# Two branch pairs of a recurrent mixer in seven products instead of eight, with the residual reloaded later

## The chip, the cores and the metric

The kernel runs on one core of a Trainium2 chip. TensorE (PE) multiplies matrices: it holds a 128x128 block of weights and streams a moving operand of up to 512 columns past it, into PSUM. VectorE (DVE) and ScalarE (ACT) do the elementwise work and are the only ones here that take results out of PSUM. GpSimd (POOL) and SyncE (SP) issue DMA transfers, each from its own queue. Every engine takes its instructions in the order of its queue and waits on semaphores for the others. The metric is device time in microseconds (us), lower is better.

## The reference

A decoder layer on 512 tokens of width 1024, in float32: a SwiGLU feed-forward (width 2816), then a mixer, then a second feed-forward, each between RMSNorms and added to the residual `h`. The mixer projects the normed input `u` once and runs two branches side by side:

```
u = rms_norm(h, mix_norm_pre)
q, k, v, xr, yr, gl = split(u @ w_in)          # xr, yr: width 1024
attn_d = dilated_attention(q, k, v) @ w_attn_branch
xc  = causal_conv4(xr) + conv_b
gate_x, gate_a = sigmoid(xc @ w_x + b_x), sigmoid(xc @ w_a + b_a)   # 4 heads of 256
a   = exp(-8 * gate_a * softplus(-a_param))
h_t = a_t * h_{t-1} + sqrt(1 - a_t^2) * gate_x * xc
rec = h_t * gelu(yr)
merged = sigmoid(gl0) * attn_d + sigmoid(gl1) * (rec @ w_rec_branch)
h = h + rms_norm(merged @ w_out, mix_norm_post)
```

The change is about `yr = u @ w_in[yr columns]`, for the first two of the four heads.

## The kernel before, in words

Precision. Every float32 operand is kept as two parts, high and low (`split`, lines 283 to 285: ACT writes the rounded high part, DVE the difference). A product is three matmuls, high x high, high x low, low x high (`mm3`, lines 297 to 299).

Weights. All weights come as one stream in order of use (`stream_plan`), in raw loads of up to 2048 columns (1 MB) into two `raw` buffers, issued by SP (line 230). `fetch` splits a tile of 128 output columns (1024 wide in memory) into one of four `w8` buffers, or a half-size one into one of two `w4` buffers.

A plain column tile is `gemm`: 8 blocks of the contraction x 3 = 24 matmuls of 128x512 into one of five PSUM tiles `acc`.

A pair of column tiles can be done in seven products (a Strassen-Winograd scheme): input and weights are cut into 2x2 quarters, the contraction in two halves and the tokens in two halves of 256, and seven products p1 to p7 of sums of quarters replace eight. A product (`seventh`, lines 616 to 618) is 4 blocks x 3 = 12 matmuls of 128x256. The forms of the input are made once per stage (`forms_of`): p1, p2, p3 are views of `u` itself, p5 and p7 lie in buffers of the pool that also holds the residual, p6 and p4 in `tx` buffers of the attention pool. The forms of the weights are made per pair by `w_forms`: with raw quarters u0, u1, g0, g1 it makes u0+u1, u0+u1+g0, u0+g0 and u0+u1+g0+g1 on DVE (512 wide each) and splits three tiles of 1024 and one of 512: one for p1 and p2 (raw g), one for p6 and p5 (the first two sums), one for p7 and p4, one for p3. Two evaluations exist: `seven`, whose results are added on DVE, and `seven_on`, which accumulates in PSUM and copies partial sums on ACT (line 631). The feed-forwards, the q/k projections and the gate of the attention branch use them.

The recurrent stage. After attention come four gate pairs (`seven`), then the attention product of eight tiles (contraction 512: 12 matmuls each), then the recurrent stage in an order written out by hand:

```
LRU_ORDER = (("conv", 0), ("branch", 0), ("branch", 1), ("conv", 1), ("gates", 0), ("branch", 2), ("conv", 2),
             ("gates", 1), ("gate1", 1), ("branch", 3), ("gates", 2), ("conv", 3), ("gate1", 2), ("gates", 3),
             ("gate1", 3))
```

`conv` of a head is two plain tiles, each evicted by DVE (line 1269), run through four taps (lines 1270 to 1272) and split into `rec`. `branch` is two plain tiles, evicted by DVE into `ge` (line 1286); after every second head ACT applies Gelu to four of them (line 1292). `gates` is the small per-head product on `rec`, and `recur` the recurrence. `rec` takes 32 KB per partition, `sig` 16 KB. Constants of the recurrence are made from `a_param` by a chain of small DVE operations and one Exp (lines 1237 to 1252).

The residual was stored in DRAM (`kept_m`) and is loaded back by POOL in four transfers of 512 KB after the last gate pair, ahead of the attention product (line 1216). It is used after the output product, much later.

Who sets the order: the program is written as one stream; a scheduler orders each engine's queue by priority, which `high_priority` raises (`AHEAD` for weight preparation, `EVAC` for evictions), and adds the waits. A new pool that lies over the memory of pools that were closed is writable when those are no longer read.

Of the kernel before, what the change touches and what calls it, by code (L numbers as in the profile page):

```python
# [10 lines left out]
F32 = mybir.dt.float32  # L11
F32R = mybir.dt.float32r
AF = mybir.ActivationFunctionType
ALU = mybir.AluOpType
# [25 lines left out]
CB = 6  # L40
GATE1 = ((), (0, 1), (2, 3, 4), (5, 6, 7))

LRU_ORDER = (("conv", 0), ("branch", 0), ("branch", 1), ("conv", 1), ("gates", 0), ("branch", 2), ("conv", 2),
             ("gates", 1), ("gate1", 1), ("branch", 3), ("gates", 2), ("conv", 3), ("gate1", 2), ("gates", 3),
             ("gate1", 3))

# [37 lines left out]
def part_blocks(a):  # L84

    return (FF_PARTS[a][1] - FF_PARTS[a][0]) // 2


def stream_plan():
# [36 lines left out]
    for h in range(NH):  # L126
        qk(h)
    for c in range(0, KC, 2):
        plan.append((("pair", 52 + c, 53 + c), 2048))
    for m in range(KC):  # L130
        plan.append((("attn", m), 512))
    for what, h in LRU_ORDER:
        if what == "gates":
            plan.append((("lru", h), 1024))
        else:
            cs = GATE1[h] if what == "gate1" else (2 * h, 2 * h + 1)
            o = {"conv": 36, "branch": 44, "gate1": 60}[what]
            for c in cs:
                plan.append((("in", o + c), 1024))
# [32 lines left out]
def hybrid_layer(ctx: ExitStack, tc: tile.TileContext, xT: bass.AP, xN: bass.AP, wst: bass.AP,  # L172
# [365 lines left out]
    def tx_slot(pool, bufs=1):  # L538
        return pool.tile([P, 2, 4, HB], F32R, name="tx", tag="tx", bufs=bufs)

    def forms_of(x, his, los, pool, copied):


        spool[0] = pool
# [2 lines left out]
        def quarter(i, j):  # L547
            return fx[:, 2 * j:2 * j + 2, i * T:i * T + T]

        def slot():  # L550
# [37 lines left out]

    spool = [None]

    def w_forms(key):

        with tc.high_priority(offset=AHEAD):
            raw = raw_of(key)
            u0, u1, g0, g1 = (raw[:, i * 512:(i + 1) * 512] for i in range(4))
            s12 = spool[0].tile([P, 2, 512], F32, name="s12", tag="s", bufs=2)
            DVE.tensor_add(s12[:, 1, :], u0, u1)  # L597
            DVE.tensor_add(s12[:, 0, :], s12[:, 1, :], g0)
            DVE.tensor_add(u0, u0, g0)
# [17 lines left out]
            PE.matmul(ps, wh, xl, start=False, stop=False, skip_group_check=True)  # L617
            PE.matmul(ps, wl, xh, start=False, stop=k == 3, skip_group_check=True)  # L618

    def seven_on(t, w, g, u):  # L620

        b, z, y, v = (acc_ps()[:, :HB] for _ in range(4))
        lo, hi = HALVES

        def copy(ps, dst=None):
            if dst is None:
                dst = tpool.tile([P, HB], F32, name="c", tag="c", bufs=CB)
            with tc.high_priority(offset=EVAC):  # L630
                ACT.activation(dst, ps, AF.Copy)  # L631
            return dst

        def sum_of(dst, ps, c):
            with tc.high_priority(offset=EVAC):
                DVE.tensor_add(dst, ps, c)
# [52 lines left out]
    def ffn(n, x, r, forms_x, apool, pss):  # L689
# [101 lines left out]
        def prod(f, w):  # L791
            g, u = tmp("g"), tmp("u")
            if f >= FIRST_ON[n]:
                v = seven_on(t, w, g, u)

                def put(dst, view):
                    for q, (h, src) in enumerate(zip(HALVES, (v, u[:, HALVES[1]]))):
                        DVE.scalar_tensor_tensor(dst[:, q] if len(dst.shape) == 3 else dst[:, h], g[:, h], -1.0, src,
                                                 op0=ALU.mult, op1=ALU.mult)
                into(f, put)  # L800
# [192 lines left out]
    ff1.close()  # L993


    with ExitStack() as mx:
        tpl = mx.enter_context(tc.tile_pool(name="attn_out", bufs=1))
        apool_cm = tc.tile_pool(name="attention", bufs=1)
# [51 lines left out]
        t, steps = forms_of(um, um_t[:2], um_t[2:], apool, False)  # L1050
# [170 lines left out]

    with ExitStack() as mx:
        rpool = mx.enter_context(tc.tile_pool(name="rec", bufs=1))
        rec_t = rpool.tile([P, 16, T], F32R, name="rec")
        rec = Act([rec_t[:, i, :] for i in range(8)], [rec_t[:, 8 + i, :] for i in range(8)])
        sig = rpool.tile([P, KC, T], F32, name="sig")
        lpool_cm = tc.tile_pool(name="lru", bufs=1)
        lpool = lpool_cm.__enter__()

# [27 lines left out]
        def pi(ap):  # L1257
            return ap.rearrange("q (p i) -> q p i", p=4)

        def conv(hd):  # L1260

            for c in (2 * hd, 2 * hd + 1):
# [109 lines left out]
        for c in range(KC):  # L1372
# [5 lines left out]
            DVE.tensor_mul(sig[:, c, :], ps, sig[:, c, :])  # L1378
            DVE.tensor_add(sig[:, c, :], sig[:, c, :], facc[:, c, :])
            split(mg.hi[c], mg.lo[c], sig[:, c, :])  # L1380


    ap2 = ctx.enter_context(tc.tile_pool(name="act2", bufs=1))
# [141 lines left out]
```

## Time and profile before

| | |
|---|---|
| median of 3 runs | 1227.53 us (1226.97 to 1227.96) |
| the profiled execution | 1227.1 us |
| its span, first to last instruction | 1225.3 us |
| granted TensorE clock, mean | 0.999 |
| busy: PE, weight loads, DVE, ACT, POOL | 99%, 90%, 80%, 64%, 2% |
| DMA, mean | 121 GB/s |

A row of the order in time is: start in us from the span's start, duration, engine, line, operation, what is written from what, shape, count; in brackets the idle time of the engine before it and what ended that. PE is the matmul, PEld the weight load that overlaps it, and SPq and POOL rows are DMA issues. Matmul durations overlap: the spacing of their starts is what a matmul costs in a row of them. "x2" merges neighbours.

### The profile page before, as it was taken

The page shows a single profiled execution, that of the slowest core. Times are in us where ns is not written, and L with a number is a line of the kernel's source. Part 1 is how long each engine was busy: PE and PEld are TensorE (multiplying, and loading weights), DVE is VectorE, ACT ScalarE, POOL GpSimd, SP SyncE. Part 2 cuts the span into 40 slices and gives each one's busy share as a digit, 9 for nine tenths or more (in the row PEclk, how much of TensorE's full clock was granted, in tenths as well). Part 3 has the DMA queues.
Part 4 walks back from the last instruction along what each step waited for, and adds up shares of the span by engine and source line. Part 5 has one row for each costly group of instructions (what it writes and reads, how often), then busy time and mean ns, then how long its engine had stood idle before and what let it go on. Part 6 is the DMA issues. An engine that isn't in the chain of part 4 may idle for free.

```text
span 1225.3 us, 19182 instructions
## 1 busy us (share of the span) xinstructions
PE 1214.1 (99%) x7700; PEld 1102.8 (90%) x7700; DVE 981.5 (80%) x1497; ACT 784.0 (64%) x1337; POOL 26.1 (2%) x51
## 2 busy tenths in 40 slices
PE   9999999999999999999999999999999999999997
PEld 8899999999878899999988888888899999999996
DVE  7988888899677587888565897785798888889975
ACT  7556777777555365665543888844566677878752
POOL 0000000000002000000000000000100000000000
PEclk9999999999999999999999999999999999999999
DMA  6223333334614222222252222234453333333341
GB/s 246 89 84 121 121 121 121 121 121 167 245 69 146 89 93 103 79 78 103 73 204 74 98 104 74 98 110 168 151 156 121 121 120 121 121 120 121 138 172 69
DMA packets 29401, 148.73 MB, mean 121 GB/s; under 512 B 3200, under 2 KB 6400, under 8 KB 15232
## 3 DMA queue, kind: packets, MB, share of 16 engines
q1 hardware_dynamic: 22032, 130.20, 29.4%
q0 software_dynamic: 7280, 17.30, 4.1%
q8 instruction: 60, 0.98, 0.3%
q14 instruction: 29, 0.24, 0.1%
HBM read 137.01 MB, written 6.29 MB: 117 GB/s over the span
## 4 chain that ended last, share of the span: by engine, by line
PE 93%; DVE 3%; ACT 2%; DMA 1%; issue 0%; DVEq 0%; ACTq 0%
PE acc L616 14%; PE acc L617 14%; PE acc L618 14%; PE acc L297 8%; PE acc L298 8%; PE acc L299 8%; PE aux L879 3%; PE aux L880 3%; PE aux L881 3%; PE acc L403 2%; PE acc L405 2%; PE acc L404 2%; PE acc L1025 1%; PE acc L1027 1%; PE acc L1026 1%; DMA raw<-in_w 1%
## 5 line engine op out<-in xcount | busy, mean ns | idle before, releaser
L285 DVE TENSOR_TENSOR w<-raw,w 128x1024 fp32r<-128x1024 f32 (+1 forms) x274 | 296.3, 1086 | 75.8 <-ACT w L284 68.8
L616 PE MATMUL acc<-big,w 128*128 128x256 f32 x1208 | 342.8, 284 | 0.4 <-ACT c L631 0.4
L617 PE MATMUL acc<-big,w 128*128 128x256 f32 x1208 | 342.7, 284 | 0.0
L618 PE MATMUL acc<-big,w 128*128 128x256 f32 x1208 | 342.4, 283 | 0.0
L284 ACT ACTIVATE w<-raw 128x1024 fp32r<-128x1024 f32 (+1 forms) x274 | 258.5, 949 | 120.1 <-PE acc L299 36.7
L616 PEld LDWEIGHTS acc<-big,w 128*128 128x128 f32 x1208 | 231.5, 192 | 2.4 <-ACT c L631 1.0
L617 PEld LDWEIGHTS acc<-big,w 128*128 128x128 f32 x1208 | 231.6, 192 | 1.4
L618 PEld LDWEIGHTS acc<-big,w 128*128 128x128 f32 x1208 | 231.6, 192 | 0.0
L616 PE MATMUL acc<-tx,w 128*128 128x256 f32 x276 | 78.5, 284 | 0.0
L617 PE MATMUL acc<-tx,w 128*128 128x256 f32 x276 | 78.1, 283 | 0.0
L618 PE MATMUL acc<-tx,w 128*128 128x256 f32 x276 | 78.1, 283 | 0.0
L879 PE MATMUL aux<-w,xf 128*128 128x512 f32 x196 | 76.4, 393 | 0.8 <-ACT w L284 0.8
L880 PE MATMUL aux<-w,xf 128*128 128x512 f32 x196 | 76.6, 391 | 0.0
L881 PE MATMUL aux<-w,xf 128*128 128x512 f32 x196 | 76.3, 389 | 0.0
L297 PE MATMUL acc<-big,w 128*128 128x512 f32 x192 | 74.7, 389 | 0.0
L298 PE MATMUL acc<-big,w 128*128 128x512 f32 x192 | 74.7, 389 | 0.0
L299 PE MATMUL acc<-big,w 128*128 128x512 f32 x192 | 74.7, 389 | 0.0
L284 ACT ACTIVATE w<-s 128x1024 fp32r<-128x1024 f32 x53 | 56.0, 1058 | 19.7 <-PE acc L618 13.9
L285 DVE TENSOR_TENSOR w<-s,w 128x1024 fp32r<-128x1024 f32 x53 | 64.6, 1218 | 4.2 <-ACT w L284 4.2
L597 DVE TENSOR_TENSOR s<-raw 128x512 f32<-128x512 f32 x53 | 36.4, 687 | 32.7 <-DMA raw<-in_w 32.7
L616 PEld LDWEIGHTS acc<-tx,w 128*128 128x128 f32 x276 | 52.9, 192 | 0.1
L617 PEld LDWEIGHTS acc<-tx,w 128*128 128x128 f32 x276 | 52.9, 192 | 0.0
(367 smaller groups left out, 2572.2 us busy)
## 6 DMA issues: line engine op xcount, KB each, us to landing
raw<-in_w SPq DMA_DIRECT2D x110, 1024.0 KB, 4.8
raw<-in_w SPq DMA_DIRECT2D x14, 512.0 KB, 3.6
big<-xf POOLq DMA_DIRECT2D x6, 512.0 KB, 3.2
gains<-in_rows POOLq DMA_DIRECT2D x5, 512.0 KB, 4.9
h<-in_x SPq DMA_DIRECT2D x8, 256.0 KB, 5.1
h<-in_xn POOLq DMA_DIRECT2D x4, 512.0 KB, 5.6
kept_m<-h POOLq DMA_DIRECT2D x4, 512.0 KB, 2.9
h<-kept_m POOLq DMA_DIRECT2D x4, 512.0 KB, 5.2
```

Of the source, the lines that this page charges most:

```text
L284: ACT.activation(dh, src, AF.Copy)
L285: DVE.tensor_sub(dl, src, dh.bitcast(F32))
L297: PE.matmul(ps, wh, xh, start=first, stop=False)
L298: PE.matmul(ps, wh, xl, start=False, stop=False)
L299: PE.matmul(ps, wl, xh, start=False, stop=last)
L597: DVE.tensor_add(s12[:, 1, :], u0, u1)
L616: PE.matmul(ps, wh, xh, start=start and k == 0, stop=False, skip_group_check=True)
L617: PE.matmul(ps, wh, xl, start=False, stop=False, skip_group_check=True)
L618: PE.matmul(ps, wl, xh, start=False, stop=k == 3, skip_group_check=True)
L879: PE.matmul(ps, xh, wh, start=first and j == 0, stop=False, skip_group_check=True)
L880: PE.matmul(ps, xh, wl, start=False, stop=False, skip_group_check=True)
L881: PE.matmul(ps, xl, wh, start=False, stop=j == 1, skip_group_check=True)
```

## The change

1. `LRU_ORDER` begins with branch 0 and branch 1, then conv 0, conv 1; the rest is as it was.
2. These two branches (`PAIRED`) are each a pair in seven products, `seven_on`, on the input forms that attention made. Their raw weights come as pairs of 2048 columns, the same bytes. `seven_on` now takes functions for its four results; the feed-forward passes its old ones, the branch copies two quarters on ACT (one with the sign turned) and adds two on DVE.
3. The first pair's weight forms are asked for behind the attention product, the second's at the head of the first branch. Their two sums use parts of `sig`, not a buffer of the closed attention pool.
4. So that the forms outlive attention, p6 and p4 of the input lie in a new pool `keep` (16 KB per partition) instead of `tx`. After the two pairs the same memory holds the second half of `rec`.
5. p5 and p7 stay in the buffers that the residual wants; its reload moves behind the two pairs.

```diff
-LRU_ORDER = (("conv", 0), ("branch", 0), ("branch", 1), ("conv", 1), ("gates", 0), ("branch", 2), ("conv", 2),
+LRU_ORDER = (("branch", 0), ("branch", 1), ("conv", 0), ("conv", 1), ("gates", 0), ("branch", 2), ("conv", 2),
...
+PAIRED = LRU_ORDER[:2]
...
         if what == "gates":
             plan.append((("lru", h), 1024))
+        elif (what, h) in PAIRED:
+            plan.append((pair_key(what, h), 2048))
...
         def slot():
-            return tx_slot(pool, 1 if copied else 2).rearrange("p s k t -> p s (k t)").rearrange(
-                "p s (b c) -> p s b c", b=2)
+            if not copied and not two:
+                v = rb()
+                two.extend(v[:, 4 * i:4 * i + 4, :].rearrange("p (s j) t -> p s j t", s=2) for i in range(2))
+            if two:
+                return two.pop(0)
+            return tx_slot(pool).rearrange("p s k t -> p s (k t)").rearrange("p s (b c) -> p s b c", b=2)
...
-    def w_forms(key):
+    def w_forms(key, s12=None):
...
-            s12 = spool[0].tile([P, 2, 512], F32, name="s12", tag="s", bufs=2)
+            if s12 is None:
+                s12 = spool[0].tile([P, 2, 512], F32, name="s12", tag="s", bufs=2)
...
-    def seven_on(t, w, g, u):
+    def seven_on(t, w, g0, g1, u0, u1):
...
         seventh(t, w, "p2", y, False)
-        ACT.activation(g[:, lo], y, AF.Silu)
+        g0(y)
         seventh(t, w, "p7", b, False)
         copy(b, v)
-        sum_of(u[:, hi], b, c5)
+        u1(b, c5)
         seventh(t, w, "p3", z, False)
-        sum_of(g[:, hi], z, c6)
-        ACT.activation(g[:, hi], g[:, hi], AF.Silu)
+        g1(z, c6)
         seventh(t, w, "p4", v, False)
-        return v
+        u0(v)
...
+    kpool_cm = tc.tile_pool(name="keep", bufs=1)
+    kpool = kpool_cm.__enter__()
+    def rec_half():
+        return kpool.tile([P, 8, T], F32R, name="rb", tag="rb")
...
-        new_h()
-        for b in range(4):
-            nc.gpsimd.dma_start(hb(b), kept_m[b])
         for c in range(KC):
             ps = acc_ps()
             gemm(ps, fetch(("attn", c)), attn)
...
-        rec_t = rpool.tile([P, 16, T], F32R, name="rec")
-        rec = Act([rec_t[:, i, :] for i in range(8)], [rec_t[:, 8 + i, :] for i in range(8)])
+        rec_t = rpool.tile([P, 8, T], F32R, name="rec")
+        rec = Act([rec_t[:, i, :] for i in range(4)], [rec_t[:, 4 + i, :] for i in range(4)])
+        rec.n = KC
         sig = rpool.tile([P, KC, T], F32, name="sig")
+        paired = {}
+        def prepare(i):
+            paired[PAIRED[i]] = w_forms(pair_key(*PAIRED[i]), sig[:, 4 + i % 2 * 2:6 + i % 2 * 2, :])
+        def pair_next(key):
+            if PAIRED.index(key) + 1 < len(PAIRED):
+                prepare(PAIRED.index(key) + 1)
+            return paired.pop(key)
+        prepare(0)
+        state["ahead"] = EVAC + AHEAD
...
+        def two_tiles(w, g, u):
+            lo, hi = HALVES
+            def up(dst, ps, sign):
+                with tc.high_priority(offset=EVAC):
+                    ACT.activation(dst[:, lo], ps, AF.Copy, scale=sign)
+            def g1(ps, c):
+                with tc.high_priority(offset=EVAC):
+                    DVE.tensor_add(g[:, hi], ps, c)
+            def u1(ps, c):
+                with tc.high_priority(offset=EVAC):
+                    DVE.scalar_tensor_tensor(u[:, hi], ps, -1.0, c, op0=ALU.mult, op1=ALU.subtract)
+            seven_on(t, w, lambda y: up(g, y, 1.0), g1, lambda v: up(u, v, -1.0), u1)
...
             gels[hd] = []
+            if ("branch", hd) in PAIRED:
+                w = pair_next(("branch", hd))
+                gels[hd] = [lpool.tile([P, T], F32, name="ge", tag="ge", bufs=6) for _ in range(2)]
+                two_tiles(w, *gels[hd])
+                return
...
-        state["ahead"] = EVAC + AHEAD
         for what, hd in LRU_ORDER:
+            if len(paired) == 0 and rec.hi[4:] == [] and (what, hd) not in PAIRED:
+                rec_t = rec_half()
+                rec.hi += [rec_t[:, i, :] for i in range(4)]
+                rec.lo += [rec_t[:, 4 + i, :] for i in range(4)]
+                new_h()
+                for b in range(4):
+                    nc.gpsimd.dma_start(hb(b), kept_m[b])
```

More of the change, by code (lines that the diff above doesn't have):

```diff
@@ L41 @@
 GATE1 = ((), (0, 1), (2, 3, 4), (5, 6, 7))
-LRU_ORDER = (("conv", 0), ("branch", 0), ("branch", 1), ("conv", 1), ("gates", 0), ("branch", 2), ("conv", 2),
+LRU_ORDER = (("branch", 0), ("branch", 1), ("conv", 0), ("conv", 1), ("gates", 0), ("branch", 2), ("conv", 2),
              ("gates", 1), ("gate1", 1), ("branch", 3), ("gates", 2), ("conv", 3), ("gate1", 2), ("gates", 3),
              ("gate1", 3))
+PAIRED = LRU_ORDER[:2]
+COLUMN = {"conv": 36, "branch": 44, "gate1": 60}
 SEVEN_STEPS = (("p1", "p7"), ("p4", "p6"), ("p5",), ("p2", "p3"))
@@ L86, in part_blocks, with pair_key @@
     return (FF_PARTS[a][1] - FF_PARTS[a][0]) // 2
+def pair_key(what, h):
+    c = COLUMN[what] + 2 * h
+    return "pair", c, c + 1
 def stream_plan():
@@ L134, in stream_plan @@
             plan.append((("lru", h), 1024))
-        else:
[L136 to L139, printed above, removed]
+        elif (what, h) in PAIRED:
+            plan.append((pair_key(what, h), 2048))
+        else:
+            for c in GATE1[h] if what == "gate1" else (2 * h, 2 * h + 1):
+                plan.append((("in", COLUMN[what] + c), 1024))
     for m in range(KC):
@@ L539, in tx_slot, with forms_of @@
         return pool.tile([P, 2, 4, HB], F32R, name="tx", tag="tx", bufs=bufs)
-    def forms_of(x, his, los, pool, copied):
+    def forms_of(x, his, los, pool, copied, rb=None):
         spool[0] = pool
@@ L548, in quarter @@
             return fx[:, 2 * j:2 * j + 2, i * T:i * T + T]
+        two = []
         def slot():
-            return tx_slot(pool, 1 if copied else 2).rearrange("p s k t -> p s (k t)").rearrange(
-                "p s (b c) -> p s b c", b=2)
+            if not copied and not two:
[4 more added lines that the diff above has]
+            return tx_slot(pool).rearrange("p s k t -> p s (k t)").rearrange("p s (b c) -> p s b c", b=2)
         x01, x10, x11 = quarter(0, 1), quarter(1, 0), quarter(1, 1)
@@ L632, in copy @@
             return dst
-        def sum_of(dst, ps, c):
-            with tc.high_priority(offset=EVAC):
-                DVE.tensor_add(dst, ps, c)
         seventh(t, w, "p1", b, True)
@@ L793, in prod, with g1, u1, u0 @@
             if f >= FIRST_ON[n]:
[L794 to L800, printed above, removed]
+                lo, hi = HALVES
+                def g1(z, c6):
+                    with tc.high_priority(offset=EVAC):
+                        DVE.tensor_add(g[:, hi], z, c6)
+                    ACT.activation(g[:, hi], g[:, hi], AF.Silu)
+                def u1(b, c5):
+                    with tc.high_priority(offset=EVAC):
+                        DVE.tensor_add(u[:, hi], b, c5)
+                def u0(v):
+                    def put(dst, view):
+                        for q, (h, src) in enumerate(zip(HALVES, (v, u[:, hi]))):
+                            DVE.scalar_tensor_tensor(dst[:, q] if len(dst.shape) == 3 else dst[:, h], g[:, h], -1.0,
+                                                     src, op0=ALU.mult, op1=ALU.mult)
+                    into(f, put)
+                seven_on(t, w, lambda y: ACT.activation(g[:, lo], y, AF.Silu), g1, u0, u1)
                 return
@@ L1048, in values @@
                 vals[g] = nv
-        t, steps = forms_of(um, um_t[:2], um_t[2:], apool, False)
+        t, steps = forms_of(um, um_t[:2], um_t[2:], apool, False, rec_half)
         values(VALUES[0], True)
@@ L1258, in pi @@
             return ap.rearrange("q (p i) -> q p i", p=4)
+        def two_tiles(w, g, u):
+            lo, hi = HALVES
+            def up(dst, ps, sign):
+                with tc.high_priority(offset=EVAC):
+                    ACT.activation(dst[:, lo], ps, AF.Copy, scale=sign)
+            def g1(ps, c):
+                with tc.high_priority(offset=EVAC):
+                    DVE.tensor_add(g[:, hi], ps, c)
+            def u1(ps, c):
+                with tc.high_priority(offset=EVAC):
+                    DVE.scalar_tensor_tensor(u[:, hi], ps, -1.0, c, op0=ALU.mult, op1=ALU.subtract)
+            seven_on(t, w, lambda y: up(g, y, 1.0), g1, lambda v: up(u, v, -1.0), u1)
         def conv(hd):
```

2 lines of the change are left out of this document (1 added, 1 removed).

## The prediction

> **What bounds the kernel now.** I read the page first, then the busy time by stretch, then the tensor engine's instructions in order of time around the change.
>
> ```profile
> span 1225.3 us, 19182 instructions
> ...
> PE 1214.1 (99%) x7700; PEld 1102.8 (90%) x7700; DVE 981.5 (80%) x1497; ACT 784.0 (64%) x1337; POOL 26.1 (2%) x51
> ...
> PE 93%; DVE 3%; ACT 2%; DMA 1%; issue 0%; DVEq 0%; ACTq 0%
> ```
>
> TensorE (PE) carries 93% of the chain that ends last. A busy PE is not proof, since matmuls overlap, so the stretch of the change comes next (columns: stretch, length, PE busy, weight loads, DVE, ACT, POOL, clock, DMA share, GB/s).
>
> ```profile
> 620.00:640.00 20.00, 20.00 (x90) 16.57 (x89) 14.55 (x32) 7.07 (x9) 0.00 (x0) 1.00 0.45 163
> 640.00:660.00 20.00, 20.00 (x90) 16.57 (x89) 12.77 (x18) 9.24 (x11) 0.00 (x0) 1.00 0.26 101
> 660.00:680.00 20.00, 20.00 (x90) 16.56 (x89) 9.46 (x11) 5.72 (x8) 0.00 (x0) 1.00 0.30 106
> ```
>
> The attention product, conv 0, branches 0 and 1 and conv 1 lie here. PE is busy 20.00 of 20.00 us at full clock; VectorE (DVE) and ScalarE (ACT) are at half or less. So only fewer or shorter matmuls can gain, and any new wait of PE costs its full length. How far apart matmuls start, of either width:
>
> ```profile
> 663.03 0.39 PE L299 MATMUL acc<-big,w 128*128 128x512 f32 x1
> ...
> 663.94 0.39 PE L297 MATMUL acc<-big,w 128*128 128x512 f32 x1
> ...
> 664.39 0.39 PE L299 MATMUL acc<-big,w 128*128 128x512 f32 x1
> ```
> ```profile
> 299.76 0.28 PE L617 MATMUL acc<-big,w 128*128 128x256 f32 x1
> ...
> 306.48 0.28 PE L616 MATMUL acc<-tx,w 128*128 128x256 f32 x1
> ```
>
> Six 512-wide steps take 1.36 us, 0.2267 each; 56 steps of 256 columns take 6.72 us, 0.120 each.
>
> **Part 1, the products: a gain of 1.60 us.** Removed are four column tiles of 24 matmuls, 96 x 0.2267 = 21.76 us. Added are two pairs of seven products with 12 half-wide matmuls each, 168 x 0.120 = 20.16 us. As PE has no idle time to give back here, 1.60 us (0.13%) is the most that the change can gain.
>
> **Part 2, the first pair's weight forms: about 1.5 us of new waits.** The sums of the forms are written into `sig`, whose pool lies over memory that attention's pools leave. In the compiled order the first sum (u0+u1) waits for the last attention product, so nothing but the split for p1 and p2 is prepared before. The rows for the walk:
>
> ```profile
> 642.38 1.10 DVE L1269 COPY xr<-acc 128x512 f32<-128x512 f32 x1 [3.06 <-PE acc L299]
> ...
> 664.14 0.69 DVE L1286 COPY ge<-acc 128x512 f32<-128x512 f32 x1 [3.06 <-PE acc L299]
> ```
> ```profile
> 630.99 1.28 DVE L1220 TENSOR_TENSOR facc<-acc,facc 128x512 f32<-128x512 f32 x2
> ...
> 692.47 0.69 DVE L1338 SCALAR_TENSOR_TENSOR gt<-th,r 128x512 f32<-128x512 f32 x1 [0.44 <-ACT r L1337]
> 693.19 0.69 DVE L1339 SCALAR_TENSOR_TENSOR r<-gt,r 128x512 f32<-128x512 f32 x1
> ```
> ```profile
> 597.93 1.06 ACT L284 ACTIVATE w<-s 128x1024 fp32r<-128x1024 f32 x1 [0.22 <-PE acc L618]
> 599.02 1.23 DVE L285 TENSOR_TENSOR w<-s,w 128x1024 fp32r<-128x1024 f32 x1 [0.26 <-ACT w L284]
> ```
> ```profile
> 178.77 0.28 PE L618 MATMUL acc<-big,w 128*128 128x256 f32 x1
> 178.96 0.39 ACT L631 ACTIVATE c<-acc 128x256 f32<-128x256 f32 x1
> ...
> 179.41 0.38 PE L616 MATMUL acc<-big,w 128*128 128x256 f32 x1 [0.36 <-ACT c L631]
> ...
> 179.63 0.28 PE L617 MATMUL acc<-big,w 128*128 128x256 f32 x1
> ```
>
> An evicting engine starts 0.20 after the next group's first matmul (664.14 against 663.94). So conv 0's first tile was issued by 642.18, and the attention product by 642.18 - 24 x 0.2267 = 636.74. Independent 512-wide DVE adds start 0.60 apart, dependent ones 0.72. A 1024-wide split takes 1.06 on ACT, and DVE's half follows 1.09 after ACT's start for 1.23. A PSUM copy takes 0.39; PE resumes 0.06 after it and loses 0.10 on the first step (0.22 for 0.12).
>
> Walk, in before's clock. p1 runs to 638.18. The compiled order puts p2 next, onto a copy of p1: 638.38 to 638.76 on ACT, PE resumes at 638.82, wait 0.64 + 0.10. On DVE: u0+u1 at 636.94, the last attention eviction 637.54, the second sum 638.14 to 638.82. ACT splits the sums from 638.85, DVE from 639.94 to 641.17. PE has done p2 and four matmuls of p5 by 640.84 and needs the low half: it resumes at 641.22, wait 0.38 + 0.10. p5 ends 642.28, p6 643.72; p7 waits for the copy after p6 (643.92 to 644.3) behind four matmuls of p3 (to 644.2), wait 0.15 + 0.10. p4 ends 648.3. Sum 1.5. Bounds: 0.8 (the p2 wait alone, fixed by the order) and 2.3, were the sums' DVE chain to shift by one 0.68 add.
>
> **Part 3, the second pair: about 1.25 us.** Its forms are in time (low half of p5's at 647.6, wanted 649.7). But ACT's queue holds, ahead of the copy that lets p6 run: conv 0's weight split, which needs the buffer that p4 frees; a copy of p4's result; then a function table for Gelu, and a Gelu. Before, the table came where nothing hurried:
>
> ```profile
> 653.30 1.06 ACT L284 ACTIVATE w<-raw 128x1024 fp32r<-128x1024 f32 x1
> 654.38 1.28 ACT L1292 ACT_TABLE_LOAD   x1
> 655.68 0.63 ACT L1292 ACTIVATE ge<-ge 128x512 f32<-128x512 f32 x1
> ```
>
> From p4's end at 648.3: split 648.5 to 649.56, copy to 649.8, table to 651.1, Gelu to 651.73, copy 651.64 to 652.02. PE has p1 and p5 to do, 2.88 us, to 651.18; p6 starts at 652.08, wait 0.90 + 0.10. p7's copy stands behind conv 0's second split, which waits for p6: 0.14 + 0.10. Bounds: 0 if the Gelus slipped behind, 2.0 if the second split held p7 for its whole 1.06.
>
> The Trainium skill, ScalarE: Activation LUTs, What ACT_TABLE_LOAD costs, charges each switch the load and a drain of about 1380 ns, 2.66 us together. The rows above show the Gelu 0.02 after the load, so the measurement decides; by the page this wait would be 1.38 longer.
>
> **Part 4, the residual's reload: about 0.9 us.** Four 512 KB loads on POOL's queue leave 611, where no raw weights travelled, for the moment p5 (first two) and p7 (last two) of the second pair free their buffers. p5 ends at 651.18, so two are issued at 651.4. SP issues conv 1's raw weights at 651.45, when the second pair's last form is split. ACT's split of them stands ahead of the copy that p4 needs.
>
> ```profile
> 622.25 0.33 SPq L230 DMA_DIRECT2D raw<-in_w  x1
> ...
> 1181.52 0.33 SPq L230 DMA_DIRECT2D raw<-in_w  x1
> ```
> ```profile
> DMA to landing us min/median/max: 4.7/4.8/5.3
> ```
> ```profile
> 627.02 2.53 ACT L284 ACTIVATE w<-raw 128x1024 fp32r<-128x1024 f32 x3 [0.33 <-DMA raw<-in_w]
> ```
> ```profile
> 1176.29 1.07 POOL L1398 DMA_DIRECT2D h<-kept  x2 [17.83 <-PE acc L618]
> 1177.85 1.05 POOL L1398 DMA_DIRECT2D h<-kept  x2 [0.49 <-PE acc L618]
> ```
> ```profile
> DMA to landing us min/median/max: 6.7/6.7/6.7
> ```
>
> A raw load lands 4.75 after its issue (622.25 to 627.0; the middle fence is all loads from 590 to 700). The one issued at 1181.52, soon after four such reloads, took 6.7 (last fence). Undisturbed it lands at 656.2: split 1.06, copy 0.39, p4 could go at 657.65, and PE wants it at 658.2: no wait. At 5.9 to 6.4, my estimate from 4.75 and 6.7 with only two reloads ahead, it can go at 658.8 to 659.3: 0.6 to 1.1, with the restart 0.9 in the middle. Bounds 0 and 1.5 (6.7). The other two reloads meet weights not needed before the gates at 682.
>
> **Part 5, what costs nothing.** Raw bytes and SP's issues are the same. The added forms and evictions are 4 us on DVE and 4 us on ACT per pair, inside stretches where both are half idle; without that cover they would cost as in parts 2 and 3. Conv 0 comes 22 us later, but its last tile is done 10.9 us (conv 1) before gates 0 wants it, against 6 us of eviction and taps. The Exp table for the recurrence constants moves up between the last two gate pairs' copies: c1 of the last pair goes from 606.57 to about 607.5, just before p6 wants it; bounds 0 and 0.5, taken 0.1.
>
> **Sum.** -1.60 + 1.5 + 1.25 + 0.9 + 0.1 = +2.1 us. From there to the end the order is unchanged and PE-bound. The profiled execution took 1227.1 (span 1225.3), 0.4 below the median of 1227.53: 1229.2 in its terms, 1229.6 against the median.
>
> **The rivals.**
> - All hidden: ACT and DVE keep ahead, as in the feed-forward pairs where 56 steps ran unbroken. Net -1.6, 1225.9. Against it: the first sum cannot start before PE is done with attention. Chance 0.07 for anything down to there.
> - No collision: reload and raw weights do not disturb each other. Net +1.2, 1228.7. For it: 4.75 to 5.3 on most loads. Chance 0.25.
> - Slower for certain: the collision is total, the raw load lands 7.1 after issue (the reloads' 1 MB is moved first, half of the 4.75 more), p4 waits 1.9, net +3.1, 1230.7. It decides from a landing 6.4 after issue on. For it: 6.7 at 1181.5. Chance 0.20. The Trainium skill, DMA: Bandwidth & Descriptors, Queues, rings and completion order, says that a DMA engine takes turns between the queues packet by packet; that would be half a collision, near the forecast's case.
> - A drain as long as the load (1.28) follows the table switch in ACT's queue: net +3.4, 1230.9, slower. The Gelu 0.02 behind the load speaks against it. Chance 0.02. It is the rule of the skill's page in part 3.
>
> **How the numbers follow.** The forecast, net +1.2 to +2.9 round 1229.6, has 0.43. A measurement of this kernel can tell about 0.2%, 2.45 us, from no change; a third of that case (0.15) lies beyond it. Slower: 0.15 + 0.20 + 0.02 = 0.37. Faster by 0.2% needs more than the whole gain of part 1, 0.03 for what I overlook. Same: 0.60. The range goes from halfway into the hidden case, 1227.0, to beyond the total collision, 1231.8; the forecast's own is 1228.7 to 1230.4.
>
> **What would show it.** In the profile after: 168 matmuls of 256 at 0.12 in this stage; PE waiting for ACT's copy before p2, for DVE's low half before p5, and for ACT behind a table load before the second p6; the first DVE sum about 0.2 after the last attention product; the raw load issued with the reloads landing 5.9 to 6.4 later; nothing new after the second pair. I am wrong if these waits sum to under 1.6 or over 4.1, or if PE waits elsewhere.

## The result and the profile after

The changed kernel takes 1229.94 us (median of 13 runs, 1229.04 to 1230.94), the kernel before 1227.70 in the runs beside it: ratio 1.0021, 95% interval 1.0014 to 1.0028, so 1.7 to 3.4 us slower. The forecast was +2.1 us. The sum came out; two of its terms did not, and they happened to offset each other.

The page of the changed kernel (span 1228.1 us), the line of busy times that answers to that of before:

```profile
PE 1214.4 (99%) x7772; PEld 1104.2 (90%) x7772; DVE 988.9 (81%) x1509; ACT 790.0 (64%) x1353; POOL 26.1 (2%) x51
```

PE's share of the chain that ends last fell from 93% to 88%. That line can't tell the kernels apart: it is 81% in run e1 below, whose instructions are those of the changed kernel in the same order, and 83% in h2, the fastest of all. The stretches show where PE is held up:

```profile
620.00:640.00 20.00, 19.54 (x94) 16.34 (x93) 10.92 (x16) 5.05 (x8) 0.00 (x0) 1.00 0.30 105
640.00:660.00 20.00, 18.80 (x151) 18.01 (x151) 14.74 (x20) 14.27 (x23) 2.16 (x4) 1.00 0.49 179
```

PE was busy 20.00 of 20 us in each of these before; now 19.54 and 18.80. The holes, in PE's order in time (a 256-wide step is 0.12 when nothing holds it, a 512-wide one 0.227):

```profile
608.24 0.28 PE L633 MATMUL acc<-big,w 128*128 128x256 f32 x1
608.46 0.39 PE L633 MATMUL acc<-rb,w 128*128 128x256 f32 x1
...
637.42 0.28 PE L633 MATMUL acc<-big,w 128*128 128x256 f32 x1
...
638.74 0.28 PE L635 MATMUL acc<-big,w 128*128 128x256 f32 x1
639.47 0.39 PE L633 MATMUL acc<-big,w 128*128 128x256 f32 x1 [0.46 <-ACT acc L647]
...
641.37 0.28 PE L635 MATMUL acc<-big,w 128*128 128x256 f32 x1
641.92 0.38 PE L635 MATMUL acc<-big,w 128*128 128x256 f32 x1 [0.27 <-DVE w L295]
...
644.77 0.66 PE L633 MATMUL acc<-big,w 128*128 128x256 f32 x2
645.27 0.28 PE L634 MATMUL acc<-big,w 128*128 128x256 f32 x1
...
651.74 0.28 PE L635 MATMUL acc<-big,w 128*128 128x256 f32 x1
652.94 0.38 PE L633 MATMUL acc<-rb,w 128*128 128x256 f32 x1 [0.93 <-ACT acc L647]
...
655.79 0.28 PE L635 MATMUL acc<-big,w 128*128 128x256 f32 x1
656.05 0.39 PE L633 MATMUL acc<-big,w 128*128 128x256 f32 x1
...
660.46 0.40 PE L307 MATMUL acc<-big,w 128*128 128x512 f32 x1
```

(The row marked x2 is two steps, 0.24 when nothing holds them; the next starts 0.50 later.) The two pairs run from 637.42 to 660.46, 23.04 us, where 168 steps need 20.16: 2.88 us of waits, against plain tiles of 21.76. No step between 656.27 and 660.46 is late, so the wait that part 4 put before the second pair's last product is not there. The page's busy shares hide all this: PE is "99%" in both kernels.

One more loss lies 144 us later, where the product on `rec` meets the last splits of the recurrence. The kernel before, then the changed one:

```profile
801.30 0.39 PE L297 MATMUL acc<-rec,w 128*128 128x512 f32 x1
801.61 0.50 PE L298 MATMUL acc<-rec,w 128*128 128x512 f32 x1
...
803.99 0.50 PE L298 MATMUL acc<-rec,w 128*128 128x512 f32 x1
```
```profile
803.29 0.39 PE L307 MATMUL acc<-rb,w 128*128 128x512 f32 x1
804.01 0.50 PE L308 MATMUL acc<-rb,w 128*128 128x512 f32 x1 [0.33 <-DVE rb L295]
...
806.38 0.50 PE L308 MATMUL acc<-rb,w 128*128 128x512 f32 x1
```

Before, the first of the two late steps (801.61, and the one at 803.99) came 0.31 after its neighbour; now (804.01 and 806.38) it comes 0.72 after it. The steps in between are the same, so 0.41 is lost.

To compare kernels below the scatter of whole runs, I take one stretch of PE's order: from the last scores of attention to the step behind the second of these late splits. It is 567.04 to 804.32 before, 237.28 us, and 567.51 to 806.72 after, 239.21: +1.93. Of the spans' difference (2.8) another 0.47 lies ahead of 567, where every engine has the same order in both kernels, and 0.4 behind 806. That is scatter: in the runs below the stretch begins anywhere from 566.26 to 568.73, and from its end to the last instruction, where PE's order is the same in all fourteen kernels, the time is 420.96 to 421.66 us. The stretch itself repeated within 0.05 us in the one kernel that was profiled twice (e1 below). Differences of a few tenths are therefore taken from the late steps themselves, and the length of the stretch only confirms them.

### The profile page after: what moved, and what is told of

Its sections match the earlier page's. It is cut to its first block, busy times and chain, and to the rows that moved or that the text cites. A ratio compares the mean times of both kernels' runs of the same rounds, so it can differ in the third digit from the quotient of the medians.

```text
span 1228.1 us, 19351 instructions
## 1 busy us (share of the span) xinstructions
PE 1214.4 (99%) x7772; PEld 1104.2 (90%) x7772; DVE 988.9 (81%) x1509; ACT 790.0 (64%) x1353; POOL 26.1 (2%) x51
## 4 chain that ended last, share of the span: by engine, by line
PE 88%; DVE 5%; ACT 4%; DMA 1%; issue 1%; SPq 0%; DVEq 0%; ACTq 0%
PE acc L633 14%; PE acc L635 14%; PE acc L634 14%; PE acc L308 6%; PE acc L309 6%; PE acc L307 6%; PE aux L902 3%; PE aux L903 3%; PE aux L904 3%; PE acc L414 2%; PE acc L413 2%; PE acc L415 2%; DVE w L295 1%; PE acc L1055 1%; PE acc L1056 1%; PE acc L1057 1%
## 5 line engine op out<-in xcount | busy, mean ns | idle before, releaser
L633 PE MATMUL acc<-big,w 128*128 128x256 f32 x1248 | 354.5, 284 | 0.9 <-ACT acc L647 0.5
L635 PE MATMUL acc<-big,w 128*128 128x256 f32 x1248 | 353.7, 283 | 0.3 <-DVE w L295 0.3
L634 PE MATMUL acc<-big,w 128*128 128x256 f32 x1248 | 353.9, 284 | 0.0
L633 PEld LDWEIGHTS acc<-big,w 128*128 128x128 f32 x1248 | 239.1, 192 | 3.6 <-ACT c L647 1.3
L634 PEld LDWEIGHTS acc<-big,w 128*128 128x128 f32 x1248 | 239.2, 192 | 1.5
L635 PEld LDWEIGHTS acc<-big,w 128*128 128x128 f32 x1248 | 239.2, 192 | 0.5 <-DVE w L295 0.5
L307 PE MATMUL acc<-big,w 128*128 128x512 f32 x160 | 62.3, 389 | 0.0
L308 PE MATMUL acc<-big,w 128*128 128x512 f32 x160 | 62.3, 389 | 0.0
L309 PE MATMUL acc<-big,w 128*128 128x512 f32 x160 | 62.2, 389 | 0.0
L647 ACT ACTIVATE c<-acc 128x256 f32<-128x256 f32 x74 | 28.2, 381 | 36.0 <-PE acc L635 35.7
L677 ACT ACTIVATE c<-acc 128x256 f32<-128x256 f32 x72 | 27.2, 379 | 31.6 <-PE acc L635 30.2
L810 ACT ACTIVATE g<-g 128x256 f32<-128x256 f32 x35 | 14.5, 416 | 51.0 <-DVE g L809 51.0
L308 PE MATMUL acc<-xf,w 128*128 128x512 f32 (+1 forms) x136 | 46.2, 340 | 0.3 <-DVE xf L385 0.3
L309 PE MATMUL acc<-xf,w 128*128 128x512 f32 (+1 forms) x136 | 46.1, 339 | 0.0
```

The costliest lines, as they stand in the source:

```text
L307: PE.matmul(ps, wh, xh, start=first, stop=False)
L308: PE.matmul(ps, wh, xl, start=False, stop=False)
L309: PE.matmul(ps, wl, xh, start=False, stop=last)
L633: PE.matmul(ps, wh, xh, start=start and k == 0, stop=False, skip_group_check=True)
```

## The experiments

The table gives every run: the stretch against 237.28, and the timed ratio to the kernel before with its 95% interval. A ratio is good to about 0.1%, 1.1 us; the stretch, from one profile each, tells apart what the ratios can't.

| run | stretch | against before | ratio (interval) |
|---|---|---|---|
| the changed kernel | 239.21 | +1.93 | 1.0021 (1.0014 to 1.0028) |
| e1 reload moved in the program | 239.16 | +1.88 | 1.0014 (1.0004 to 1.0023) |
| e2 Gelus later | 238.04 | +0.76 | 1.0008 (0.9999 to 1.0017) |
| e3 sums early | 237.66 | +0.38 | 1.0004 (0.9995 to 1.0012) |
| e4 order alone | 237.70 | +0.42 | 1.0003 (0.9994 to 1.0012) |
| f1 sums and Gelus | 236.44 | -0.84 | 0.9995 (0.9986 to 1.0003) |
| f2 conv first | 236.30 | -0.98 | 0.9996 (0.9988 to 1.0005) |
| f3 low halves on POOL | 241.11 | +3.83 | 1.0036 (1.0024 to 1.0049) |
| f4 all three | 238.38 | +1.10 | 1.0007 (0.9997 to 1.0016) |
| h1 POOL, heads 0 and 1 | 238.49 | +1.21 | 1.0009 (1.0000 to 1.0018) |
| h2 first order, best | 235.44 | -1.84 | 0.9983 (0.9974 to 0.9992) |
| h3 old order, best | 236.47 | -0.81 | 0.9992 (0.9983 to 1.0000) |
| h4 old order, POOL | 236.91 | -0.37 | 0.9999 (0.9990 to 1.0007) |

**e1, the reload moved in the program.**

```diff
                 rec.lo += [rec_t[:, 4 + i, :] for i in range(4)]
+            if (what, hd) == ("gates", 0):
                 new_h()
                 for b in range(4):
```

> The changed kernel with the residual's four reloads moved from behind the second pair to just ahead of gates 0, some 20 us later; nothing else moves on PE, ACT and DVE. Prediction on record (part 4): a collision of reload and conv 1's raw weights holds the second pair's last product by 0.9 us; by that, 0.9 us faster than the changed kernel. Theory after reading its trace: the raw load issued at 652.33 beside the first two reloads was split from 657.32 on, 5.0 after its issue, and PE shows no gap ahead of that product; by that, the same as the changed kernel within 0.3 us (1229.9 +- 0.3).

The edit moves the reload in the program, but it did not move it in time. POOL's queue holds nothing else in between, and the loads were issued as soon as their buffers came free, 0.02 from conv 1's raw load as in the changed kernel:

```profile
651.49 1.11 POOL L1426 DMA_DIRECT2D h<-kept_m  x2 [273.49 <-PE acc L635]
```
```profile
651.51 0.33 SPq L240 DMA_DIRECT2D raw<-in_w  x1
```

On every engine the instructions come in the order of the changed kernel. So this run does not test the collision; it is the changed kernel measured a second time. Its stretch is 0.05 shorter, with the same holes, and its ratio 0.0007 lower. What the collision cost has to be read from the changed kernel's own trace, further below.

**e2, the Gelus later.**

```diff
+            if hds == (0, 1):
+                zb = s8("zb")[:, 0:1]
+                DVE.tensor_scalar(zb, gels[1][1][:, 0:1], 0.0, None, op0=ALU.mult)
...
+                        ACT.activation(ge, ge, AF.Gelu_apprx_tanh, bias=zb)
```

> The changed kernel with the four Gelus of the two pairs made to wait for the last result of the second pair (they take a bias of zero worked out from it), so that the Gelu table load no longer stands in ACT's queue ahead of the copy that lets the second p6 run. Theory (part 3 of the prediction, and the trace: PE's step of 1.20 at 652.94 and of 0.26 at 656.05): the wait of 1.18 goes, the 0.24 before p7 stays or goes with it: 1.1 to 1.4 us faster than the changed kernel, about 1228.7. Rival: ACT's other work ahead of that copy (conv 0's weight split and the copy of p4's result) is late enough by itself, or another wait (raw weights of conv 1) takes its place: 0.4 us or less is gained.

The stretch is 1.17 shorter: the 1.18 before the second p6 is gone, the 0.24 before p7 stays. Part 3's wait is the table load and the Gelu, shown by moving them alone.

**e3, the sums early.**

```diff
-        apool_cm.__exit__(None, None, None)
         for c in range(KC):
...
+        paired = {PAIRED[0]: w_forms(pair_key(*PAIRED[0]))}
+        apool_cm.__exit__(None, None, None)
...
-        prepare(0)
```

> The changed kernel with the first pair's sums in a buffer of the attention pool, which is closed only behind the attention product; so the forms of the weights are ready before that product ends. Theory (part 2, and the trace: PE's steps of 0.73 at 639.47, 0.55 at 641.92, 0.50 for two at 645.27, against 0.12): the waits of 1.5 us in the first pair go, and perhaps the 0.2 before the gate pair's p6 with the moved Exp table: 1.2 to 1.7 us faster than the changed kernel. Rival: what is late is not the buffer but the raw weights or the ACT copy after p1, which stays: 0.7 or less is gained.

The stretch is 1.55 shorter. The first pair has one late step left, of 0.09 at its p6, and the compiled order, which had put p2 second because the other forms were late, has p5 there, which hides ACT's copy. The 0.20 at 608.46 went too (the constants' Exp is placed later), and the second p6 waits 0.12 longer. So the place of the sums, with the order that follows from it, cost the first pair's 1.5.

**e4, the order alone.**

```diff
-LRU_ORDER = (("conv", 0), ("branch", 0), ("branch", 1), ("conv", 1), ("gates", 0), ("branch", 2), ("conv", 2),
+LRU_ORDER = (("branch", 0), ("branch", 1), ("conv", 0), ("conv", 1), ("gates", 0), ("branch", 2), ("conv", 2),
```

> The kernel before with branch 0, branch 1 ahead of conv 0, conv 1, all four as plain tiles, and nothing else changed: no pairs, the residual reloaded where it was. Prediction on record (part 5): conv 0 later by 22 us is harmless; by that, 0 against the kernel before. Theory after reading the trace: four conv tiles in a row take DVE and ACT 5.66 us each against PE's 5.44, so gates 0 is evicted 0.4 us later against PE than before, the dense elementwise work of the recurrent stage never makes it up, and PE waits 0.4 us longer at its end (804.01) for the last split of rec: 0.3 to 0.6 us slower than the kernel before.

The stretch is 0.42 longer (the times alone could not tell), and the loss stands where the changed kernel has it:

```profile
802.45 0.50 PE L298 MATMUL acc<-rec,w 128*128 128x512 f32 x1 [0.34 <-DVE rec L285]
```

So the new order costs 0.4 without any pair. The cause begins with conv 0 and conv 1, now four tiles in a row. DVE's evictions of them in the changed kernel:

```profile
666.13 1.09 DVE L1328 COPY xr<-acc 128x512 f32<-128x512 f32 x1 [2.89 <-PE acc L309]
...
671.39 0.69 DVE L295 TENSOR_TENSOR rec<-sig,rec 128x512 fp32r<-128x512 f32 x1 [0.57 <-ACT rec L294]
672.00 1.07 DVE L1328 COPY xr<-acc 128x512 f32<-128x512 f32 x1
...
677.66 1.06 DVE L1328 COPY xr<-acc 128x512 f32<-128x512 f32 x1
...
683.31 1.06 DVE L1328 COPY xr<-acc 128x512 f32<-128x512 f32 x1
```

They come 5.87, 5.66 and 5.65 apart, PE's tiles 24 x 0.2267 = 5.44. In DVE's queue the next eviction stands behind the low half of the last result, which waits 0.57 for ACT. From there the lag goes on: the first gates are issued by PE 1.99 later than before and evaluated by ACT 2.37 later, and each of ACT's steps up to 796 keeps that 2.37 to 2.40. The rows, of the changed kernel and of before:

```profile
682.25 0.39 PE L307 MATMUL aux<-rec,w 128*128 128x512 f32 x1
685.24 1.28 ACT L1386 ACT_TABLE_LOAD   x1
```
```profile
680.26 0.39 PE L297 MATMUL aux<-rec,w 128*128 128x512 f32 x1
682.87 1.28 ACT L1322 ACT_TABLE_LOAD   x1
```

**f1, both edits of e2 and e3.**

```diff
+        paired = {PAIRED[0]: w_forms(pair_key(*PAIRED[0]))}
...
+                        ACT.activation(ge, ge, AF.Gelu_apprx_tanh, bias=zb)
```

> The changed kernel with both edits: the first pair's sums in the attention pool and the Gelus behind the second pair. In the stretch from attention's last scores (567.04 before) to the last late split of rec (804.32 before), the kernel before took 237.28 us, the changed one 239.21, the sums edit alone 237.66, the Gelu edit alone 238.04. Theory: the two waits are independent, so the stretch takes 1.93 - 1.55 - 1.17 = 0.8 us less than before, 236.5, and the kernel 0.8 us less than the kernel before (ratio 0.9994). Rival: with the forms and the Gelus out of the way another supply (conv 1's raw weights, issued at 652.33 and split at 657.32) holds the second pair: less than half of it is gained, 237.2 or more.

236.44 against 236.5 expected: the two waits are independent.

**f2, the order of before with pairs and later Gelus.**

```diff
-PAIRED = LRU_ORDER[:2]
+PAIRED = (("branch", 0), ("branch", 1))
...
-        prepare(0)
...
+                if (what, hd) == ("conv", 0):
+                    prepare(0)
```

> The changed kernel in the order of before (conv 0, then the two paired branches, then conv 1), the sums in their place in sig, the Gelus behind the second pair. Conv 0 covers the preparation of the first pair's forms, and only two conv tiles stand in a row. Theory: the 1.5 us of the first pair and the 0.4 us at the end of the recurrent stage go, but conv 0's taps and splits now stand in ACT's queue ahead of the first pair's copies: a wait of about 0.5 comes back before its p6, and 0.2 to 0.3 before p7; stretch 236.2 to 237.0 against 237.28 before. Rival: the order was the price throughout (the conv work ahead costs more than it covers): 237.3 or more.

236.30, near the lower end: nothing waits before the first p6 (0.16 before the same pair's p4 instead, 0.24 before the second p7 as forecast, and still the 0.20 before the gate pair's p6), and the end of the recurrent stage is as in the kernel before. Conv 0 covers the forms as well as e3's buffer does.

**f3 and f4, conv's low halves on POOL** (f4: with the edits of f1).

```diff
-                    split(rec.hi[c], rec.lo[c], xc)
+                    ACT.activation(rec.hi[c], xc, AF.Copy)
+                    nc.gpsimd.tensor_sub(rec.lo[c], xc, rec.hi[c].bitcast(F32))
```

> The changed kernel with the low halves of conv's result (eight 512-wide differences in the recurrent stage) taken by POOL instead of DVE, so that DVE does not wait for ACT between one conv tile's taps and the next one's eviction. Theory: DVE's cycle per conv tile falls from 5.66 to under 5.44, the lag of the four tiles in a row goes, and the wait at the end of the recurrent stage (0.49 and 0.20 in the changed kernel) falls by 0.4 or more: stretch 238.8 or less against 239.21. Rival: the lag is not from the conv tiles, or the wait at the end is set by the last head's own chain: 239.1 to 239.3; or POOL is so slow that gates wait for it: longer than 239.3.

> The three edits together: sums in the attention pool, Gelus behind the second pair, low halves of conv's result on POOL. Theory: the gains add up, and the products' 1.60 is then nearly all there: stretch 235.7 to 236.1 against 237.28 before, the kernel 1.2 to 1.6 us faster than the kernel before (ratio about 0.9988). Rival: as soon as PE runs on, DVE's and ACT's chain of the recurrent stage bounds the stretch, and the gain comes back as a longer wait at its end: 236.5 or more.

Both came out longer than expected: f3 1.90 longer than the changed kernel, f4 1.94 longer than f1. f3's DVE, POOL and PE:

```profile
671.24 1.12 DVE L1328 COPY xr<-acc 128x512 f32<-128x512 f32 x1 [0.76 <-PE acc L309]
...
676.68 1.11 DVE L1328 COPY xr<-acc 128x512 f32<-128x512 f32 x1 [0.75 <-PE acc L309]
```
```profile
671.11 1.30 POOL L1334 TENSOR_TENSOR rec<-sig,rec 128x512 fp32r<-128x512 f32 x1 [11.80 <-ACT rec L1333]
...
766.28 4.33 POOL L1334 TENSOR_TENSOR rb<-sig,rb 128x512 fp32r<-128x512 f32 x1 [3.89 <-ACT rb L1333]
```
```profile
770.67 0.50 PE L308 MATMUL aux<-rb,w 128*128 128x512 f32 x1 [0.64 <-POOL rb L1334]
```

The first half of the theory holds: the evictions come 5.44 apart, and DVE now waits for PE. But the same difference that takes POOL 1.30 in the first heads takes 4.33 for the last, where DVE is busy all 4.33 us with the recurrence and weight splits, and gates 3 waits for it; PE then waits 1.03 and 0.50 at the end. A new wait took the old one's place, in f4 as well. Whether the lag sets the end stayed open; the next run asks it.

**h1, POOL for heads 0 and 1 alone.**

```diff
+                    low = nc.gpsimd if hd < 2 else DVE
+                    low.tensor_sub(rec.lo[c], xc, rec.hi[c].bitcast(F32))
```

> The changed kernel with the low halves of conv's result on POOL for heads 0 and 1 alone (1.30 us each on POOL in the run with all heads, where DVE's evictions then followed PE at 5.44), heads 2 and 3 as they were. Theory: the lag of the four conv tiles in a row (0.4 us against PE at gates 0) goes, and with it 0.4 of the wait at the end of the recurrent stage: stretch 238.8 or less against 239.21. Rival: the wait at the end is made by the last heads' own chain and not by what gates 0 started with: 239.1 to 239.3.

The stretch is 0.72 shorter than the changed kernel's. DVE's evictions of the four conv tiles come 5.44 apart, and the last three wait 0.75 for PE. The first of the two late steps is no longer late, and the second is 0.11 less so. So a lag of 0.4 that arose at 672 to 683 is what PE pays at 804; the lag that before has from its two tiles in a row costs it some 0.3 there as well.

**h2, the order of the change with everything mended:** the edits of f1 and h1, and conv 0's weight splits placed below the pair's copies.

```diff
+            state["ahead"] = AHEAD if (what, hd) == ("conv", 0) else EVAC + AHEAD
```

> The order of the changed kernel with the sums in the attention pool, the Gelus behind the second pair, conv 0's weight splits below the pair's copies, and the low halves of heads 0 and 1 on POOL. Theory: from 236.44 (sums and Gelus) the 0.24 before the second p7 and 0.4 at the end go: stretch 235.7 to 235.9, 1.4 to 1.6 us less than the kernel before (ratio 0.9987 to 0.9989). Rival: a wait takes their place (raw weights of conv 1, or the last heads' chain): 236.3 or more.

The stretch is 235.44, 1.84 less than before and a little below the range expected, and the ratio 0.9983 (0.9974 to 0.9992): faster than both kernels. The stretch of the pairs, to set against the one above:

```profile
640.00:660.00 20.00, 20.00 (x163) 19.75 (x162) 15.35 (x42) 12.13 (x22) 2.17 (x4) 1.00 0.52 193
```

PE is busy 20.00 of 20 again, and the 168 steps of the pairs take 20.22 us. The gain is more than part 1's 1.60 because 0.33 of the waits that the kernel before has at the end of the recurrent stage goes too. That part comes from the low halves on POOL, not from the products; no run gave them to the kernel before alone.

**h3 and h4, the order of before with everything mended** (h4: POOL for heads 0 and 1 too).

```diff
+        xz = s8("xz")[:, 0:1]
+        DVE.tensor_scalar(xz, facc[:, KC - 1, 0:1], 0.0, None, op0=ALU.mult)
+        ACT.activation(ex, ab, AF.Exp, bias=xz)
...
+            state["ahead"] = AHEAD if (what, hd) == ("conv", 1) else EVAC + AHEAD
```

> The order of before with pairs and later Gelus (236.30), and two more edits: the recurrence constants' Exp waits for the last attention product (a bias of zero made from it), and conv 1's weight splits stand below the pair's copies. Theory: the 0.19 before the gate pair's p6 and the 0.24 before the second p7 go: stretch 235.8 to 236.0, 1.3 to 1.5 us less than the kernel before (ratio 0.9988 to 0.9990). Rival: the table switches for Exp now fall into conv 0's and the first pair's ACT queue and the wait comes back before the first p6: 236.2 or more.

> The kernel of the run h3 with the low halves of heads 0 and 1 on POOL. Theory: two conv tiles in a row lag DVE by 0.46 at the second tile in the kernel before too, so 0.1 to 0.2 of the wait that it has at the end of the recurrent stage goes: stretch 0.1 to 0.2 less than h3's. Rival: that wait is the last heads' own: the same as h3 within 0.05.

h3 missed its expectation, by the wait that part 4 had forecast for the changed kernel. Its raw load for conv 1 was issued at 659.20, two reloads 2.1 us behind it; it landed 6.4 after its issue, ACT's split of it stood ahead of the copy that the last product needs, and PE paid 0.79:

```profile
665.67 1.06 ACT L294 ACTIVATE w<-raw 128x1024 fp32r<-128x1024 f32 x1 [1.82 <-DMA raw<-in_w]
```
```profile
667.33 0.38 PE L633 MATMUL acc<-rb,w 128*128 128x256 f32 x1 [0.53 <-ACT acc L647]
```

Whether the reloads made this load late is open. What moved from its issue to 663.25, just ahead of the reloads' first packet (packets, MB, share; q1 is SP's queue, q8 the queue of instructions):

```profile
q1 hardware_dynamic: 118, 0.96, 69.4%
q8 instruction: 1, 0.02, 1.8%
```

So 118 of the load's 128 packets of 8 KB had started before a reload moved anything, and a packet of instructions went beside them. In the same profile a raw load issued at 824.65, beside one such packet and no reload at all, landed after 7.2:

```profile
q8 instruction: 1, 0.02, 1.2%
...
raw<-in_w SPq DMA_DIRECT2D x1, 1024.0 KB, 7.2
```

Raw loads of 1 MB that travelled with neither, and with no other raw load, took at most 4.94 in all fourteen profiles. The instruction packet is thus a rival to the reloads as the cause, and no run separates the two.

The stretch of h4 can't be read for its question: its ACT queue came out in another order, with waits of 0.92, 0.25 and 0.38 in the pairs. Its end can. Of the two late steps the first is no longer late, nor is the step behind it, and the second takes 0.32 against h3's 0.42, some 0.3 less together, while h3, with its 0.79 of waits ahead of conv 1, kept both. So in the order of before, too, part of the wait at the end is the lag of the conv tiles, as the theory had it and not the rival.

## Why the prediction was right in the sum, and where it was wrong

Part 1 holds: 168 steps at 0.12. h2 shows the gain once almost nothing stands in its way (20.22 us against 21.76).

Part 2, taken as 1.5: 0.72 before p2 (forecast 0.74), 0.53 before the low half of p5 (0.48), 0.26 before p7 (0.25), 1.51 in all, each with the 0.10 that the first step behind a wait takes longer. The walk held because everything in it was an order, read from the compiled queues, and durations, read from rows. The first sum started 0.20 after the next issue, as laid down:

```profile
637.62 0.69 DVE L614 TENSOR_TENSOR sig<-raw 128x512 f32<-128x512 f32 x1 [2.03 <-PE acc L309]
```

Part 3, taken as 1.25: 1.18 and 0.24. The queue was as walked, the split, the copy, the table, the Gelu:

```profile
650.31 0.36 ACT L1307 ACTIVATE ge<-acc 128x256 f32<-128x256 f32 x1
650.69 1.28 ACT L1356 ACT_TABLE_LOAD   x1
651.99 0.63 ACT L1356 ACTIVATE ge<-ge 128x512 f32<-128x512 f32 x1
652.52 0.37 ACT L647 ACTIVATE acc<-acc 128x256 f32<-128x256 f32 x1
```

The Gelu starts 0.02 behind the load, so the rival with a drain is excluded here too.

Part 4, taken as 0.9, was nothing: PE has no late step before the second pair's last product. The step that failed is the landing "at 5.9 to 6.4, my estimate from 4.75 and 6.7". The issues came together as laid down, 0.02 apart:

```profile
652.33 0.33 SPq L240 DMA_DIRECT2D raw<-in_w  x1
```
```profile
652.31 1.11 POOL L1425 DMA_DIRECT2D h<-kept_m  x2 [273.48 <-PE acc L635]
```
```profile
h<-kept_m POOLq DMA_DIRECT2D x2, 512.0 KB, 6.4
raw<-in_w SPq DMA_DIRECT2D x1, 1024.0 KB, 5.0
```

The raw load landed after 5.0, the reloads after 6.4: I had the right pair and the delay on the wrong one. What moved in the 4.0 us from 652.4 on, and in the 2.0 us after that (q1 is SP's queue, q0 POOL's; packets, MB, share):

```profile
q1 hardware_dynamic: 126, 1.03, 77.4%
q0 software_dynamic: 1, 0.00, 0.2%
```
```profile
q0 software_dynamic: 211, 0.80, 97.4%
```

The one queue was served after the other, not in shares, so the mix that the estimate supposed was not there. It is not that reloads start slowly. With no raw load in flight they move 1.03 MB in as long a time, as in the kernel before in the 4.0 us from 611.2 on:

```profile
q0 software_dynamic: 275, 1.03, 69.1%
```

And it repeats: in e1, e2, f3 and h1, where the two were issued 0.02 apart as well, q0 moved at most 4 packets in those 4.0 us, and the raw load landed after 4.8 to 5.1.

The Trainium skill, DMA: Bandwidth & Descriptors, Queues, rings and completion order, lets an engine take turns between queues packet by packet, and a packet is there a group of typically 9 to 17 descriptors. The raw load here is 128 pieces of 8 KB, eight to each of the 16 engines, so by an estimate from that page one turn could take in the load's whole share of an engine. The stretch therefore does not contradict the page; the half collision that the prediction drew from it did not come.

The 6.7 at 1181.5 that I drew the estimate from was a load issued behind reloads that were already under way, which is another case. The changed kernel has that case too: its next raw load, issued at 657.01 while the reloads moved, landed after 6.2, and no step of PE waited for it.

Part 5, taken as 0.1 with "nothing new after the second pair", was 0.61. The Exp's table cost 0.20 before the gate pair's p6 (at 608.46 a step of 0.22, and the next one as long). And "conv 0 comes 22 us later" was held harmless by looking at when its own last tile is done; I did not ask what four conv tiles in a row do to DVE, though the rows of before show the cycle, nor follow a lag of half a microsecond to where it is paid. The prediction also said that it would be wrong if PE waited elsewhere: at 804 it does, 0.41 longer than before, and by its own sign it is wrong there.

Sum: -1.60 + 0.20 + 1.51 + 1.42 + 0 + 0.41 = +1.94, against +1.93 in the stretch and +2.24 between the medians. That the forecast of +2.1 came out is in part luck: a term of 0.9 that was not there stood against 0.5 that was left out and 0.2 of small excess. Parts 1 to 3 alone, at 1.15, would have been 0.8 short. For part 4 the rival without a collision is what the trace shows.

## What to carry to other kernels

On a path where one engine is never idle, walk each new dependence through the compiled queues with durations from rows: the terms that were walked so came within 0.2 us, while the one term that rested on shared bandwidth was wrong by its whole size. Where work is reordered, look at what now stands back to back: a chain across two engines that is 0.2 us longer than its supplier's cycle gathers lag with each repetition, and a stage with no slack carries it to its end. And a saving in the busiest engine's own work is worth having only with its supply mended: kernels with the same products took 1.9 us more or 1.8 us less than the kernel before, depending on where a buffer of 4 KB per partition lay, when a function table was loaded, where a weight split stood in ACT's queue and which engine took four differences. Last, an edit has moved something only if the trace shows it moved: e1's reload stayed where it was.

## What was not expected of the hardware

A 128x512 difference on POOL takes 1.29 or 1.30 us in five of its eight places in run f3, where DVE was copying out of PSUM or partly idle. It takes 2.18, 3.04 and 4.33 us in the other three, where DVE was busy the whole time, mostly with instructions that read two tiles. DVE's own instructions are longer there too: one that otherwise takes 0.74 took 1.77. And one raw load and two reloads, 1 MB on each queue, issued 0.02 us apart on two queues, did not share the DMA engines: the raw load was moved before the reloads, in five profiles of five. Why the order was this one isn't settled by these runs. Nor is what makes a raw load land after 6 us or more with no other load about: in these profiles it was seen only beside a packet of instructions.
